# Decoder layer in emulated float32 on one core: the two down projections as seven half-size block products

## The chip, the cores and the metric

The kernel runs on one core of a Trainium2 chip. The metric is the device time of one execution in microseconds (us). A core has a matrix engine (PE, or TensorE), the vector engine DVE, the scalar engine ACT, the general engine POOL (GpSimd) and the engine SP, which here only issues transfers. Each works through its own instructions in a fixed order and waits on semaphores for the others; a transfer queued on SP holds everything queued behind it while it waits.

## The reference, cut to what matters

1024 tokens, width 1024, one layer: a SwiGLU half step, a token mixer, a second SwiGLU half step, each with a norm before and a norm behind it, and with shift, scale and gate rows made from a vector c.

```python
D_MODEL, SEQ, D_FF = 1024, 1024, 2816
def swiglu(h, w_gate, w_up, w_down):
    return (jax.nn.silu(h @ w_gate) * (h @ w_up)) @ w_down
# x += 0.5 * gate * rms_norm(swiglu(modulate(rms_norm(x))))   once before, once behind the mixer
# the nine rows (shift, scale, gate) x 3 are silu(c) @ w_mod + b_mod, w_mod being 1024 x 9216
```

The down projection is act (1024 x 2816) by w_down (2816 x 1024), in float32.

## The kernel before, in words

**Float32 by splits.** An operand is split into a high part, cast on ACT, and a low part, which DVE makes by a subtraction (`split`, L75; `psplit`, L79, makes it on POOL). `mm3` (L102) then issues three matmuls: high by high, high by low, low by high. A matmul here is always 128x128 by 128x512.

**Stages, in us of the profiled execution.** Opening to 130 (first gate/up products among it), gate/up 1 to about 490, its down projection to about 750, mixer to 1890, gate/up 2 to 2265, its down to about 2500, the last norm to the end.

**Gate/up** (`gate_up`, L252) is already made of seven half-size products. It goes over NB = 11 blocks of 256 columns of D_FF; each has seven steps i = 0..6 of 2 x 4 mm3. Step 2 makes the sums of weight blocks on POOL (L286 to L289), each step has weights split (`wl` on DVE), and DVE adds the products together out of PSUM (L343, L346). ACT takes the silu, POOL multiplies (L351), and SP stores one 128x512 tile of activations to DRAM for each of i = 1, 4, 5, 6 (L353). Operands are prepared LOOK steps ahead. Between the steps of the blocks from EARLY = 5 on, a generator `mod_rest` is advanced FILL = 2 times a step: it makes the rows for shift, scale and gate. For each half row it loads eight 128x512 pieces of w_mod (`wr`, four buffers, on SP) and accumulates them on DVE (`macc`, L183 and L185); then come a split, two matmuls with ones (bank `mo`) and one or two tiny DVE instructions on 1x512 (`junk`, L194 to L199). What is not done by the end of gate/up 1 runs in the second pass of down 1.

**Down** (`down`, L368) first loads all activations into SBUF (`act`, 44 loads of 256 KB, four chunks ahead of the products) and keeps them. It makes two passes over 22 chunks of 128 rows of w_down: output columns 0 to 511 for all eight token tiles, then columns 512 to 1023 for tiles 0 to 3 and for tiles 4 to 7. Each PSUM bank is read by ACT (sum of squares) and by DVE (times the gate row, `evac`, L363). Then `post1` or `post2` takes the norm of a half (four token tiles), adds the residual (`residual`, L1155) and, in the first layer, makes the mixer's input (`prenorm`, L1162). The last half's norm runs behind the last product. The mixer's first weights (`wc0r`) are loaded and split there (`wc0h` on ACT, `wc0l` on POOL).

**Order.** A scheduler builds each engine's order from the program order and each engine keeps it; tiles come from pools with fixed numbers of buffers, and a load into a buffer waits until the last reader of the tile before has ended.

Of the kernel before, what the change touches and what calls it, by code (L numbers as in the profile page):

```python
# [10 lines left out]
F32 = mybir.dt.float32  # L11
# [9 lines left out]
D = 1024  # L21
# [8 lines left out]
FILL = 2  # L30
NPT, NAP = 6, 6
# [8 lines left out]
class Layer:  # L40
# [125 lines left out]
    def mod_rest(self, pool, rows):  # L166

        nc, i = self.nc, self.i
        gains = {4: "g_pre_mix", 7: "g_pre_ffn2", 2: "g_post_ffn1", 5: "g_post_mix", 8: "g_post_ffn2"}
        for v in (2, 3, 4, 5, 6, 7, 8):  # L170
            for h in range(2):
                c0 = v * D + h * 512
                acc = pool.tile([P, 512], F32, name="macc")
                for k in range(8):
                    r = pool.tile([P, 512], F32, name="wr", tag="wr", bufs=4)
                    nc.sync.dma_start(r, i["w_mod"][0, k * P:(k + 1) * P, c0:c0 + 512])
                    if k == 4:
                        bt, gt = rows[0][0:1, :], rows[1][0:1, :]
                        nc.sync.dma_start(bt, i["b_mod"][0:1, c0:c0 + 512])
                        if v in gains:  # L180
                            nc.sync.dma_start(gt, i[gains[v]][0:1, h * 512:(h + 1) * 512])
                    if k == 0:
                        nc.vector.tensor_scalar(acc, r, self.scol[:, 0:1], None, op0=ALU.mult)  # L183
                    else:
                        nc.vector.scalar_tensor_tensor(acc, r, self.scol[:, k:k + 1], acc, op0=ALU.mult, op1=ALU.add)  # L185
                    yield
                b = self.bank("mo", tag=self.mo)
                ah = pool.tile([P, 512], F32R, name="mah", tag="wr", bufs=4)
                al = pool.tile([P, 512], F32R, name="mal", tag="wr", bufs=4)
                self.split(ah, al, acc)  # L190
                nc.tensor.matmul(b, self.ones, ah, start=True, stop=False)
                nc.tensor.matmul(b, self.ones, al, start=False, stop=True)
                if v in (4, 7):
                    nc.vector.scalar_tensor_tensor(bt, b[0:1, :], 1.0, bt, op0=ALU.add, op1=ALU.add)  # L194
                    nc.vector.tensor_mul(bt, bt, gt)
                else:
                    nc.vector.tensor_add(bt, b[0:1, :], bt)  # L197
                    if v in gains:
                        nc.vector.scalar_tensor_tensor(bt, bt, 1.0 if v == 5 else 0.5, gt, op0=ALU.mult, op1=ALU.mult)  # L199
                nc.sync.dma_start(self.rows[v:v + 1, h * 512:(h + 1) * 512], bt)  # L200
                yield
# [50 lines left out]
    def gate_up(self, W, raws, pools, V, wg, wu, actd):  # L252
# [44 lines left out]

        prepped = set()
# [18 lines left out]
        def steps(order, filler=None, ahead=()):  # L317
# [4 lines left out]
            for s, (b, i) in enumerate(order):  # L322
# [4 lines left out]
                for m in range(2):  # L327
# [5 lines left out]
                    if m == 0 and i < 4:  # L333
                        if i == 0 and b in early and b > 2:
                            tiles[b, i] = [pools["x"].tile([P, 512], F32, name="px", tag="wr", bufs=4) for _ in range(2)]
# [32 lines left out]
    def down(self, W, W2, wd, room, actd, y, G, junk, ss, post, filler=None):  # L368

        nc = self.nc  # L370
        NF = DFF // P
        tags = ("tr", "tr", "o", "gg", "pj", "pj", "s", "pt")
        got = [0]
        bg = iter(())
        for dh, tiles in ((0, range(8)), (1, range(4)), (1, range(4, 8))):
            bk = {t: self.bank("dn", tag=tags[t]) for t in tiles}
            halves = sorted({t // 4 for t in tiles})
            late, last = [], dh == 1
            nlate = (1, LATE + (W2 is not None) * 2 if tiles[-1] == 7 else 1)[dh]

            def mul(t, c, w, a):
                ts = slice((t % 4) * P, (t % 4 + 1) * P)
                ah, al = a[t // 4]
                self.mm3(bk[t], ah[:, ts], al[:, ts], w[0], w[1], c == 0, c == NF - 1)

            for c in range(NF):
                while got[0] < min(NF, c + 4):
                    for h in range(2):
                        nc.sync.dma_start(room[got[0]][h], actd[got[0], :, h * 512:(h + 1) * 512])
                    got[0] += 1  # L390
                if c % 2 == 0:
                    r = self.raw([P, 2, 512], "rd")
                    nc.sync.dma_start(r, wd[0, c * P:(c + 2) * P, dh * 512:(dh + 1) * 512]
# [1014 lines left out]
```

## Time and profile before

| | |
|---|---|
| median of three runs | 2530.2 us |
| the three runs | 2525.76, 2530.2, 8078.31 us |
| the profiled execution's own time | 2522.99 us |
| its span, first to last instruction | 2521.2 us |
| mean granted TensorE clock | 0.970 |
| busy: PE, DVE, ACT, POOL | 94%, 64%, 43%, 38% |
| matmuls | 11279 |

"Busy" says how much of the span an engine had an instruction in flight. As an average over unlike stages it doesn't tell what bounds any of them: for that, the busy times are taken stage by stage, and then the waits in the stage. A wait is named as "who waits <- who ended last", so that "PE gu L105 <- DVE wl L77" is PE standing until DVE had made the low part of a weight.

### The profile page before, as it was taken

Reading aid. Unit: us, or ns where it says so; the run is one execution under the profiler, and the core shown is the slowest. Engines: PE = TensorE matmul, PEld = TensorE weight load, DVE = VectorE, ACT = ScalarE, POOL = GpSimd, SP = SyncE. Lnnn points to the kernel's source line nnn. Section 1 sums busy time; section 2 is a strip of 40 time slices with the busy share of each in tenths; the row PEclk is TensorE's granted clock in tenths of the full one; section 3 lists DMA queues with packets and bytes.
Section 4 is the critical chain, followed back from the end, with each engine's and each line's share of the span. In section 5 each row is a group of like instructions: output and inputs, shape, how many; then the busy total and the mean of one; then the engine's idle time right before and its main releaser. Section 6 shows DMA issues by size and latency. Waiting matters only on the chain.

```text
span 2521.2 us, 33999 instructions
## 1 busy us (share of the span) xinstructions
PE 2362.8 (94%) x11279; PEld 1983.2 (79%) x11279; DVE 1611.2 (64%) x3193; ACT 1094.4 (43%) x2342; POOL 952.4 (38%) x1109
## 2 busy tenths in 40 slices
PE   5799999999999999999998899799879999999997
PEld 4578887788878878888997777678658888888886
DVE  7866778754884245999736388874486554553455
ACT  5422323233454355777453466623443333333443
POOL 5775555400005423432243144601587454430012
PEclk9899999999999999999998699999889999999999
DMA  9234555761633223513311422154234322253134
GB/s 282 85 109 134 152 153 159 241 219 51 193 131 119 74 88 109 187 30 89 117 31 59 118 70 65 44 200 167 84 113 130 96 76 92 80 193 108 52 108 150
DMA packets 229803, 300.04 MB, mean 119 GB/s; under 512 B 23606, under 2 KB 144342, under 8 KB 229628
## 3 DMA queue, kind: packets, MB, share of 16 engines
q1 hardware_dynamic: 228988, 296.80, 37.3%
q8 instruction: 90, 1.47, 0.2%
q10 hardware_dynamic: 640, 1.07, 0.1%
q14 instruction: 85, 0.70, 0.1%
HBM read 233.98 MB, written 63.83 MB: 118 GB/s over the span
## 4 chain that ended last, share of the span: by engine, by line
PE 69%; DVE 13%; DMA 8%; issue 4%; POOL 3%; ACT 2%; SPq 0%; DVEq 0%; POOLq 0%; ACTq 0%
PE gu L104 7%; PE gu L105 7%; PE gu L106 7%; PE dn L105 6%; PE dn L106 6%; PE dn L104 6%; DMA wr<-in_w_mod_dram 3%; PE gpj L104 2%; PE gpj L105 2%; PE gpj L106 2%; PE bq L104 2%; DVE macc L185 1%; PE bq L106 1%; PE bq L105 1%; DVE wl L77 1%
## 5 line engine op out<-in xcount | busy, mean ns | idle before, releaser
L104 PE MATMUL gu<-V,wh 128*128 128x512 f32 x1232 | 488.9, 397 | 18.9 <-ACT wh L76 9.3
L105 PE MATMUL gu<-V,wl 128*128 128x512 f32 x1232 | 487.9, 397 | 6.9 <-DVE wl L77 6.5
L106 PE MATMUL gu<-V,wh 128*128 128x512 f32 x1232 | 483.1, 395 | 4.5 <-DVE V L77 4.5
L77 DVE TENSOR_TENSOR wl<-rw,wh 128x512 fp32r<-128x512 f32 x232 | 215.3, 931 | 134.8 <-PE gu L105 95.4
L104 PEld LDWEIGHTS gu<-V,wh 128*128 128x128 f32 x1232 | 235.0, 191 | 73.3 <-ACT wh L76 11.3
L105 PEld LDWEIGHTS gu<-V,wl 128*128 128x128 f32 x1232 | 234.8, 191 | 60.4 <-DVE wl L77 9.4
L106 PEld LDWEIGHTS gu<-V,wh 128*128 128x128 f32 x1232 | 233.6, 190 | 56.6 <-DVE V L77 7.1
L105 PE MATMUL dn<-dh,al 128*128 128x512 f32 x704 | 275.3, 391 | 1.2 <-DVE al L77 1.1
L106 PE MATMUL dn<-dl,ah 128*128 128x512 f32 x704 | 274.0, 390 | 0.0
L104 PE MATMUL dn<-dh,ah 128*128 128x512 f32 x704 | 253.4, 391 | 6.5 <-DVE junk L197 6.5
L76 ACT CAST wh<-rw 128x512 fp32r<-128x512 f32 x232 | 140.1, 618 | 213.0 <-PE gu L106 124.9
L351 POOL TENSOR_TENSOR p<-p 128x512 f32<-128x512 f32 x86 | 129.9, 1511 | 246.5 <-ACT wh L81 78.5
L343 DVE TENSOR_TENSOR p<-gu,p 128x512 f32<-128x512 f32 x252 | 170.0, 681 | 68.9 <-PE gu L106 42.9
L76 ACT CAST ah<-act 128x512 fp32r<-128x512 f32 x176 | 107.4, 621 | 182.9 <-PE dn L105 132.9
L77 DVE TENSOR_TENSOR al<-act,ah 128x512 fp32r<-128x512 f32 x176 | 118.0, 689 | 81.5 <-PE dn L105 42.8
L104 PEld LDWEIGHTS dn<-dh,ah 128*128 128x128 f32 x704 | 132.3, 188 | 34.5 <-DVE junk L197 7.0
L105 PEld LDWEIGHTS dn<-dh,al 128*128 128x128 f32 x704 | 132.6, 188 | 29.9 <-DVE al L77 2.6
L77 DVE TENSOR_TENSOR dl<-rd,dh 128x512 fp32r<-128x512 f32 x132 | 91.2, 692 | 100.9 <-PE dn L105 52.5
L106 PEld LDWEIGHTS dn<-dl,ah 128*128 128x128 f32 x704 | 132.5, 188 | 27.6
L349 ACT ACTIVATE p<-p 128x512 f32<-128x512 f32 x86 | 54.4, 633 | 211.0 <-DVE p L343 161.7
L185 DVE SCALAR_TENSOR_TENSOR macc<-wr,scol,macc 128x512 f32<-128x512 f32 x98 | 93.3, 952 | 51.2 <-DMA wr<-in_w_mod_dram 50.5
L76 ACT CAST dh<-rd 128x512 fp32r<-128x512 f32 x132 | 81.6, 618 | 82.9 <-PE dn L105 71.5
(465 smaller groups left out, 5473.9 us busy)
## 6 DMA issues: line engine op xcount, KB each, us to landing
rd<-in_w_down_dram SPq DMA_DIRECT2D x66, 512.0 KB
wr<-in_w_mod_dram SPq DMA_DIRECT2D x112, 256.0 KB
rw<-in_w_gate_dram SPq DMA_DIRECT2D x44, 512.0 KB
rw<-in_w_up_dram SPq DMA_DIRECT2D x44, 512.0 KB
act<-act SPq DMA_DIRECT2D x88, 256.0 KB
act<-p SPq DMA_DIRECT2D x86, 256.0 KB
wm<-in_w_mod_dram SPq DMA_DIRECT2D x32, 256.0 KB
x<-xt SPq DMA_DIRECT2D x16, 512.0 KB
```

The costliest lines, as they stand in the source:

```text
L76: self.nc.scalar.copy(hi, src)
L77: self.nc.vector.tensor_sub(lo, src, f(hi))
L104: mm(out, ah, bh, start=start, stop=False)
L105: mm(out, al, bh, start=False, stop=False)
L106: mm(out, ah, bl, start=False, stop=stop)
L185: nc.vector.scalar_tensor_tensor(acc, r, self.scol[:, k:k + 1], acc, op0=ALU.mult, op1=ALU.add)
L343: nc.vector.tensor_tensor(x[m], bk, y[m], op=ALU.add)
L349: nc.scalar.activation(x[0], x[0], AF.Silu)
L351: nc.gpsimd.tensor_tensor(x[1], x[1], x[0], op=ALU.mult)
```

## The change

**Down as seven products.** act is cut into 2 x 2 blocks (token halves by even and odd chunks of D_FF) and w_down likewise (chunk parity by column halves). `down` now makes seven products of 11 chunks x 4 token tiles x mm3, in the order `prods`, with two sets of four banks in turn. Both operands are loaded from DRAM for two chunks at a time (`ra`, `rd`, 512 KB each), and split by ACT and DVE. Behind each product, `o1` to `o7` combine the banks into y: ACT copies, DVE additions, POOL subtractions; where a block of y is done, its square goes to ACT and its gate multiplication to POOL or DVE. The norm of half 0 runs under the last two products, that of half 1 behind the last.

**Operands of the seven products.** `operands` makes the sums of activation blocks at steps 1, 4, 5 and 6 of each gate/up block (three on POOL, one on DVE) and stores 7 tiles a block (8 in an early block, one of which is loaded again) instead of 4. `mix_down` makes the sums of w_down blocks in quarters of 128x256: for each of 11 chunk pairs and two column quarters q, two loads, four subtractions (POOL for q = 0, DVE for q = 1) and four stores, out of one buffer `wx`. It is advanced beside the steps of gate/up.

**Rows of shift, scale and gate.** `mod_rest` accumulates in place in the loaded tile (`wr`, five buffers), ends a half row DELAY = 3 loads later, and is advanced once a step in the early blocks too; in down 1 it is advanced once a chunk in the first five products.

```diff
+DELAY = 3
...
+                    acc = r
...
+        def operands(b, i, x):
+            out = lambda n, t: nc.sync.dma_start(ad[n, b], t)
+            sub = lambda E, o, x, y: E.tensor_tensor(o, x, y, op=ALU.subtract)
+            if i == 1:
+                tiles[b, "21"] = x
+                if b in early:
+                    out(7, x[1])
+                return
+            if i != 1:
+                tiles[b, {4: "22", 5: "12", 6: "11"}[i]] = x
+                out({4: 1, 5: 2, 6: 0}[i], x[1])
+            if i == 4:
...
+                nc.gpsimd.tensor_tensor(x[0], tiles[b, "21"][1], x[1], op=ALU.add)
+                out(3, x[0])
+            if i == 6:
+                (s1, _), (s3, a21), (s4, a12), (s2, a11) = (tiles[b, n] for n in ("22", "21", "12", "11"))
+                sub(nc.gpsimd, s2, s1, a11)
+                out(4, s2)
+                sub(nc.vector, s3, a11, a21)
+                out(5, s3)
+                sub(nc.gpsimd, s4, a12, s2)
+                out(6, s4)
...
-                            ff, h = {1: (0, 0), 4: (1, 0), 5: (1, 1), 6: (0, 1)}[i]
-                            nc.sync.dma_start(actd[2 * b + ff, :, h * 512:(h + 1) * 512], x[1])
-                if filler is not None and b >= len(early):
-                    for _ in range(FILL):
+                            operands(b, i, x)
+                if filler is not None:
+                    for _ in range(FILL if b >= len(early) else 1):
                         next(filler, None)
...
+    def mix_down(self, pool, wd, out):
+        for j in range(NB):
+            for q in range(2):
+                E = nc.vector if q else nc.gpsimd
+                r = pool.tile([P, 2, 2, 256], F32, name="wx", tag="wx", bufs=1)
+                for e in range(2):
+                    nc.sync.dma_start(r[:, e], wd[0, (2 * j + e) * P:(2 * j + e + 1) * P, :]
+                                      .rearrange("p (c f) -> p c f", c=2)[:, :, q * 256:(q + 1) * 256])
+                yield
...
+                sub(b11, b12, b11)
+                sub(b12, b22, b12)
+                sub(b22, b22, b11)
+                sub(b21, b22, b21)
+                yield
+                for n, t in enumerate((b11, b22, b12, b21)):
+                    nc.sync.dma_start(out[n, j, :, q * 256:(q + 1) * 256], t)
+                yield
...
+        def o6(b, t):
+            add(C(1, 2, t), C(1, 1, t), b)
+            nc.gpsimd.tensor_tensor(C(2, 1, t), C(1, 2, t), C(2, 1, t), op=ALU.subtract)
...
+        def o3(b, t):
+            add(C(1, 2, t), C(1, 2, t), b)
+            normed(1, 2, t, nc.gpsimd)
+        prods = [(0, wb[0, 0], o1), (1, T(3), o4), (4, T(1), o6), (3, T(0), o5), (5, T(2), o7),
+                 (2, wb[1, 0], o2), (6, wb[1, 1], o3)]
+        for n, (A, B, end) in enumerate(prods):
...
+            for j in range(NB):
+                if j % 2 == 0:
+                    m = min(2, NB - j)
+                    r = [raws(n, j).tile([P, 2, 512], F32, name=x, tag="raw") for x in ("rd", "ra")]
+                    nc.sync.dma_start(r[1][:, 0:m], ad[A, j:j + m].rearrange("j p f -> p j f"))
+                    nc.sync.dma_start(r[0][:, 0:m], B[:, j:j + m])
+                w, a = ([Ws(n, j).tile([P, 512], F32R, name=f"{m}{x}", tag="w") for x in "hl"] for m in "da")
+                self.split(a[0], a[1], r[1][:, j % 2])
+                self.split(w[0], w[1], r[0][:, j % 2])
...
+                if end in (o2, o3):
+                    next(bg, None)
+                elif filler is not None:
+                    next(filler, None)
...
+            for t in range(4):
+                for x in late:
+                    mul(t, *x)
+                end(bk[t], t)
...
-        with pool("cp") as cp, pool("wa", 16) as W, pool("ce") as ce, pool("r2", 4) as L.rawp, pool("tb") as tb:
+        with pool("wa", 16) as W, pool("r2", 4) as L.rawp, pool("cp") as cp, pool("ce") as ce, pool("tb") as tb:
```

**How the orders move.** DVE in gate/up 1, between two additions out of PSUM of block 6, before (`macc` are the row accumulations, `p` the additions, `wl` the weight splits):

```order
L343 TENSOR_TENSOR p3_2583<-gu_2570,p2_2539 128x512
L77 TENSOR_TENSOR wl0_2606<-rw01_2265,wh0_2605 128x512
L185 SCALAR_TENSOR_TENSOR macc_2750<-wr_2895,scol_99,macc_2750 128x512
L185 SCALAR_TENSOR_TENSOR macc_2750<-wr_2898,scol_99,macc_2750 128x512
L343 TENSOR_TENSOR p3_2583<-gu_2585,p2_2539 128x512
L77 TENSOR_TENSOR wl1_2610<-rw11_2267,wh1_2609 128x512
L185 SCALAR_TENSOR_TENSOR macc_2750<-wr_2938,scol_99,macc_2750 128x512
L343 TENSOR_TENSOR p0_2439<-gu_2617,p3_2583 128x512
```

The same stretch with the change (accumulation is into `wr_1923` and `wr_2354`, `wx` are the sums of w_down):

```order
L382 TENSOR_TENSOR p3_2495<-gu_2482,p2_2438 128x512
L203 SCALAR_TENSOR_TENSOR wr_1923<-wr_2242,scol_100,wr_1923 128x512
L78 TENSOR_TENSOR wl0_2526<-rw01_2155,wh0_2525 128x512
L419 TENSOR_TENSOR wx_2573<-wx_2573 128x256
L188 TENSOR_TENSOR junk0_96<-mo_2134,junk0_96 1x512
L203 SCALAR_TENSOR_TENSOR wr_1923<-wr_2294,scol_100,wr_1923 128x512
L382 TENSOR_TENSOR p3_2495<-gu_2497,p2_2438 128x512
L190 SCALAR_TENSOR_TENSOR junk0_96<-junk0_96,junk1_97 1x512
L201 TENSOR_SCALAR wr_2354<-wr_2354,scol_100 128x512
L78 TENSOR_TENSOR wl1_2530<-rw11_2157,wh1_2529 128x512
L203 SCALAR_TENSOR_TENSOR wr_1923<-wr_2347,scol_100,wr_1923 128x512
L203 SCALAR_TENSOR_TENSOR wr_2354<-wr_2404,scol_100,wr_2354 128x512
```

Between the two additions on p3, four instructions besides the split now stand where two stood, and the row accumulations of two half rows overlap.

SP in gate/up 1 with the change (before, only the `wr`, `rw` and `act1` rows are there):

```order
L415 DMA wx_2407<-in_w_down1_dram 128x2x256
L198 DMA wr_1523<-in_w_mod_dram 128x512
L311 DMA act1_85<-px_443 128x512
L426 DMA wx1_86<-wx_2407 128x256
L426 DMA wx1_86<-wx_2407 128x256
L198 DMA wr_1566<-in_w_mod_dram 128x512
L311 DMA act1_85<-px_442 128x512
L198 DMA wr_1610<-in_w_mod_dram 128x512
L426 DMA wx1_86<-wx_2407 128x256
L426 DMA wx1_86<-wx_2407 128x256
L311 DMA act1_85<-p3_2116 128x512
L415 DMA wx_2471<-in_w_down1_dram 128x2x256
```

The next load of `wx` stands behind the four stores out of the same buffer, and the weight and row loads queue among them.

DVE near the end of down 1 with the change, where the sixth product's banks are added (`y1 <- dn`) and the seventh's operands (`dl`, `al`) are split:

```order
L78 TENSOR_TENSOR al_6377<-ra_6371,ah_6376 128x512
L441 TENSOR_TENSOR y1_4537<-y1_4537,dn_5916 128x512
L1253 SCALAR_TENSOR_TENSOR xt_6163<-y0_4538,sums_4548,xt_6163 128x1024
L441 TENSOR_TENSOR y1_4537<-y1_4537,dn_5917 128x512
L441 TENSOR_TENSOR y1_4537<-y1_4537,dn_5918 128x512
L441 TENSOR_TENSOR y1_4537<-y1_4537,dn_5919 128x512
L78 TENSOR_TENSOR dl_6375<-rd_6370,dh_6374 128x512
```

The residual of the fourth token tile (`xt_6163`) stands ahead of a split that a later chunk needs; before, it stood among the splits of the second pass, without an addition behind it.

## Rows read from the trace of the kernel before

**Rows 1.** By stage: start:end, length, busy (xinstructions) by engine, clock, DMA share, GB/s

```profile
130.00:290.00 160.00, 159.63 (x691) 129.97 (x692) 101.37 (x138) 46.94 (x79) 102.51 (x71) 1.00 0.43 130
290.00:490.00 200.00, 198.87 (x861) 161.13 (x860) 164.50 (x210) 58.97 (x107) 109.62 (x68) 1.00 0.54 166
490.00:515.00 25.00, 18.45 (x74) 14.69 (x73) 12.33 (x20) 5.81 (x10) 3.26 (x3) 0.86 1.04 377
515.00:750.00 235.00, 234.82 (x1044) 193.25 (x1043) 153.13 (x287) 101.96 (x191) 0.00 (x0) 1.00 0.42 138
750.00:780.00 30.00, 23.06 (x115) 20.99 (x114) 24.95 (x82) 14.26 (x35) 17.23 (x28) 0.89 0.43 149
...
1890.00:2265.00 375.00, 374.64 (x1647) 309.60 (x1646) 206.51 (x268) 119.30 (x198) 187.60 (x141) 1.00 0.34 109
2265.00:2500.00 235.00, 233.86 (x1032) 193.31 (x1031) 111.51 (x168) 94.31 (x174) 18.96 (x38) 1.00 0.32 107
```

**Rows 2.** Costliest groups of the page: count | busy, mean ns | idle

```profile
L105 PE MATMUL dn<-dh,al 128*128 128x512 f32 x704 | 275.3, 391 | 1.2 <-DVE al L77 1.1
```

**Rows 3.** Waits of PE, 100 to 2522: total us, times, longest

```profile
PE dn L104 <- DVE junk L197: 6.5, 1, 6.5
PE gu L105 <- DVE wl L77: 6.5, 6, 2.1
...
PE cpj L104 <- ACT wc0h L81: 3.9, 1, 3.9
```

**Rows 4.** Waits, 300 to 480

```profile
DVE macc L185 <- DMA wr<-in_w_mod_dram: 20.0, 19, 2.2
...
DVE macc L183 <- DMA wr<-in_w_mod_dram: 12.1, 5, 3.9
```

**Rows 5.** DVE's groups by shape, 300 to 500

```profile
L185 DVE SCALAR_TENSOR_TENSOR macc<-wr,scol,macc 128x512 f32<-128x512 f32 x48 | 50.7, 1056 | 20.5 <-DMA wr<-in_w_mod_dram 20.3
L77 DVE TENSOR_TENSOR wl<-rw,wh 128x512 fp32r<-128x512 f32 x56 | 46.3, 829 | 0.0
L343 DVE TENSOR_TENSOR p<-gu,p 128x512 f32<-128x512 f32 x59 | 39.6, 679 | 0.0
L77 DVE TENSOR_TENSOR mal<-macc,mah 128x512 fp32r<-128x512 f32 x7 | 6.3, 893 | 0.9 <-ACT mah L76 0.7
...
L199 DVE SCALAR_TENSOR_TENSOR junk<-junk,junk 1x512 f32<-1x512 f32 x3 | 4.2, 1407 | 0.0
...
L197 DVE TENSOR_TENSOR junk<-mo,junk 1x512 f32<-1x512 f32 x5 | 3.3, 670 | 0.0
```

**Rows 6.** POOL's groups by shape, 300 to 500

```profile
L289 POOL TENSOR_TENSOR rw<-rw,rw 128x512 f32<-128x512 f32 x9 | 16.1, 1792 | 4.6 <-DVE wl L77 4.6
```

**Rows 7.** DVE's groups, 540 to 620, where POOL is idle

```profile
L77 DVE TENSOR_TENSOR al<-act,ah 128x512 fp32r<-128x512 f32 x29 | 18.9, 688 | 26.4 <-ACT ah L76 26.4
...
L185 DVE SCALAR_TENSOR_TENSOR macc<-wr,scol,macc 128x512 f32<-128x512 f32 x3 | 2.3, 752 | 2.4 <-DMA wr<-in_w_mod_dram 2.4
```

**Rows 8.** The chain that ended last, 380 to 520: start, us, what

```profile
408.02 4.11 DMA wr<-in_w_mod_dram
...
490.84 6.38 DMA act<-act
497.28 5.90 DMA rd<-in_w_down_dram
```

**Rows 9.** Waits of SP's queue, 120 to 560

```profile
SPq L353 <- POOL p L351: 113.8, 27, 9.2
...
SPq L176 <- DVE macc L185: 48.2, 47, 2.6
```

**Rows 10.** DVE's groups, gate/up 2, 1900 to 2260

```profile
L77 DVE TENSOR_TENSOR wl<-rw,wh 128x512 fp32r<-128x512 f32 x112 | 106.5, 951 | 123.2 <-PE gu L105 94.2 <-issue 12.4 <-ACT p L349 9.6
```

**Rows 11.** DVE's timeline, 753 to 780: start, us

```profile
755.94 1.26 DVE L1160 SCALAR_TENSOR_TENSOR xt<-y,sums,xt 128x1024 f32<-128x1024 f32 x1
```

**Rows 12.** DVE's timeline, 2505 to 2522

```profile
2511.48 0.68 DVE L366 TENSOR_TENSOR y<-dn,G 128x512 f32<-128x512 f32 x1
```

More of the change, by code (lines that the diff above doesn't have):

```diff
@@ new lines, in end @@
+        def end(v, h, acc):
+            c0 = v * D + h * 512
+            bt, gt = rows[0][0:1, :], rows[1][0:1, :]
+            nc.sync.dma_start(bt, i["b_mod"][0:1, c0:c0 + 512])
+            if v in gains:
+                nc.sync.dma_start(gt, i[gains[v]][0:1, h * 512:(h + 1) * 512])
+            b = self.bank("mo", tag=self.mo)
+            ah, al = (pool.tile([P, 512], F32R, name=f"ma{n}", tag="wr", bufs=5) for n in "hl")
+            self.split(ah, al, acc)
+            nc.tensor.matmul(b, self.ones, ah, start=True, stop=False)
+            nc.tensor.matmul(b, self.ones, al, start=False, stop=True)
+            if v in (4, 7):
+                nc.vector.scalar_tensor_tensor(bt, b[0:1, :], 1.0, bt, op0=ALU.add, op1=ALU.add)
+                nc.vector.tensor_mul(bt, bt, gt)
+            else:
+                nc.vector.tensor_add(bt, b[0:1, :], bt)
+                if v in gains:
+                    nc.vector.scalar_tensor_tensor(bt, bt, 1.0 if v == 5 else 0.5, gt, op0=ALU.mult, op1=ALU.mult)
+            nc.sync.dma_start(self.rows[v:v + 1, h * 512:(h + 1) * 512], bt)
@@ new lines, in mod_rest @@
+        late = None
+        for v, h in [(v, h) for v in (2, 3, 4, 5, 6, 7, 8) for h in range(2)]:
+            c0 = v * D + h * 512
+            for k in range(8):
+                r = pool.tile([P, 512], F32, name="wr", tag="wr", bufs=5)
+                nc.sync.dma_start(r, i["w_mod"][0, k * P:(k + 1) * P, c0:c0 + 512])
+                if k == 0:
+                    acc = r
+                    nc.vector.tensor_scalar(acc, r, self.scol[:, 0:1], None, op0=ALU.mult)
+                else:
+                    nc.vector.scalar_tensor_tensor(acc, r, self.scol[:, k:k + 1], acc, op0=ALU.mult, op1=ALU.add)
+                yield
+                if late and k == DELAY:
+                    end(*late)
+                    yield
+            late = v, h, acc
@@ L204, in turn @@
+        for _ in range(DELAY):
+            yield
+        end(*late)
     def turn(self, ys, d, sh, a=None):
@@ L366, in evac @@
         self.nc.vector.tensor_tensor(y, b, g, op=ALU.mult)
-    def down(self, W, W2, wd, room, actd, y, G, junk, ss, post, filler=None):
+    def mix_down(self, pool, wd, out):
         nc = self.nc
-        NF = DFF // P
-        tags = ("tr", "tr", "o", "gg", "pj", "pj", "s", "pt")
-        got = [0]
-        bg = iter(())
[L375 to L393, printed above, removed]
-                                      .rearrange("(k p) f -> p k f", p=P))
-                pool = W2 if W2 is not None and nlate > 1 and NF - nlate <= c < NF - nlate + 2 else W
-                w = [pool.tile([P, 512], F32R, name=f"d{n}", tag="w") for n in "hl"]
-                self.split(w[0], w[1], r[:, c % 2])
-                a = {}
-                for h in halves:
-                    a[h] = [pool.tile([P, 512], F32R, name=f"a{n}", tag="w") for n in "hl"]
-                    self.split(a[h][0], a[h][1], room[c][h])
-                if c >= NF - nlate:
-                    late.append((c, w, a))
@@ L404, in down @@
                     continue
[L405 to L407 removed]
+                for t in range(4):
+                    mul(t, j, w, a)
+                if end in (o2, o3):
                     next(bg, None)
[L409 to L414 removed]
@@ L422, in down @@
-        for _ in bg:
+                end(bk[t], t)
+            if end is o7:
+                bg = post(0)
+        for _ in post(1):
             pass
@@ L1182, in layer_kernel, with both @@
     sums = lambda: [L.const.tile([P, 4], F32, name="sums", bufs=8) for t in range(8)]
-    def rooms(fp):
-        r = [L.big.tile([P, 8, 512], F32, name="act", tag="big") for _ in range(4)]
-        f2 = [[fp[h].tile([P, 512], F32, name=f"act{c}{h}") for h in range(2)] for c in range(16, DFF // P)]
-        return [[r[2 * h + c // 8][:, c % 8] for h in range(2)] for c in range(16)] + f2
+    def both(a, b):
+        n = 0
+        while n < 2:
+            n = sum(next(g, 0) is not None for g in (a, b))
+            yield
+    operands = lambda n: L.dram.tile([8, NB, P, 512], F32, name=f"act{n}")
+    sums_of = lambda n: L.dram.tile([4, NB, P, 512], F32, name=f"wx{n}")
     L.turns = gu_turns()
```

150 lines of the change are left out of this document (82 added, 68 removed).

## The prediction

> **What bounds the kernel now.** I read the busy times by stage first, since a share over the whole span mixes stages with unlike limits. In both down projections PE is busy for 235 of 235 us at the full clock while DVE and ACT are at two thirds or under [rows 1]: down is bound by the number of its matmuls, and little else stands in it. Gate/up 2 is the same, with DVE busy 206.5 of 375 us. Gate/up 1 looks like that too, but from 290 to 490 DVE is at 164.5 of 200 us, and of its 35.5 idle us 32.1 are waits for pieces of w_mod [rows 1, 4]. The chain of waits confirms it: in that stretch it runs through DVE and through loads of `wr` of 4 us, not through PE [rows 8]. So PE and DVE are both nearly full there. Then I read the boundary from 490 to 515: 377 GB/s, PE busy 18.45 us, clock 0.86, the chain in loads of `act` and `rd` [rows 1, 8]. The question is whether work that down loses comes back in gate/up 1.
>
> **The change part by part.** Sums are made against the profiled execution, 2523.0 us; the median is 7.2 above it and the lowest run 2.8 above.
>
> *Fewer matmuls in down.* Before, 3 x 704 = 2112 of them [rows 2], 1056 a layer; with the change 7 x 11 x 4 x 3 = 924, so 264 fewer in all. From 515 to 750, 1044 take 235 us [rows 1], 0.2251 us each: **-59.4 us**. What feeds them: a product has 22 splits on DVE at 0.69 us [rows 7], 15 us in its 132 x 0.2251 = 29.7; additions behind a product are four to twelve, in another bank set than PE's next product. Covered, with half of DVE free.
>
> *Gate/up 1, DVE.* Counted in the order, DVE gets from the blocks behind the early ones: 25 more row accumulations at 1.056 us = 26.4; three more ends of a half row at 0.893 + 1.407 + 0.670 = 2.97, 8.9 [rows 5]; six subtractions of activation blocks, taken as 0.829 like a split in that stretch, 5.0; 24 subtractions of 128x256. Those the trace does not have. A 128x1024 instruction takes 1.26 us [rows 11] and a 128x512 one of that kind 0.752 [rows 7], so about 0.51 goes with 512 columns and 0.24 is fixed: 0.24 + 0.25 = 0.5, an estimate, x 24 = 12.0 (ends: half of 0.829, 10, and 0.829, 20). Together 52. POOL also gets about 16 sums at up to 1.79 us [rows 6] and 24 quarter sums at half of that plus, some 47 us, beside 109.6 [rows 1]. With POOL idle an accumulation takes 752 ns and a split 688; in this stretch they take 1056 and 829, while the additions out of PSUM stay at 679 [rows 5, 7]. That is 48 x 0.304 + 56 x 0.141 + 7 x 0.2 = 24 us of DVE for 109.6 us of POOL, 0.22 us for each: + 10. The Trainium skill ("SBUF - State Buffer", "Who interferes with whom") says that DVE with two SBUF inputs and GpSimd reading SBUF contend for one shared port as for a lock, the loser standing for the whole instruction; it speaks against this change. The trace agrees in kind (only the instructions with two SBUF inputs are longer) and not in size: 0.22, not one for one. By that rule the 10 us would be up to 47, a rival below.
>
> So DVE needs 164.5 + 62 = 226 us in a stretch of 200. Of its 32 us of waits half go: five buffers instead of four, and a busier DVE is waited for rather than waiting; half stay, since the loads queue on SP among twice as many transfers. 226 + 16 + the 3 other idle us = 245; less some 12 that operands prepared ahead and the early blocks take up, where DVE is busy for 101.37 of 160 us [rows 1]. **+33 us**. Low end +8: no wait left, the quarters at the low price, the rest in the early blocks. High end +55: all waits stay, quarters at 0.829. Behind a late addition out of PSUM stands the bank, so PE waits; it is already seen to wait 6.5 us for `wl` [rows 3].
>
> *Gate/up 2.* The same sums, without rows. DVE gets 44 quarters and 11 subtractions, about 32 us on 206.5 of 375, POOL 33 sums and 44 quarters, some 75 on 187.6 [rows 1]. DVE idles there 94 us waiting for PE [rows 10]: covered, **+2** (0 to +10, if that cover breaks up into pieces shorter than the sums).
>
> *Boundary to down 1.* The 44 loads of activations go; each product streams its own. 74 matmuls in 25 us are 16.7 us of work, so 8.3 were lost, 6.5 of them in one wait of PE for a `junk` of the rows [rows 1, 3]. With the change only two operands of 512 KB are wanted at once, but the last block's activations go to DRAM and back. **-5** (-9 to +5).
>
> *Residual of the fourth tile.* It stands on DVE ahead of a split and behind a load that queues on SP behind the mixer's weights, which wait for buffers that PE frees. If it is late, splits behind it are late and PE stands: a load of 4 us [rows 8] and 1.26 [rows 11], less what is split ahead. **+3** (0 to +6).
>
> *Boundary to the mixer.* Now 23.06 of 30 us [rows 1], 3.9 of it a wait for `wc0h` [rows 3]. The first mixer weights are split earlier, and half of the small norm instructions go to POOL: **-3** (-8, above the whole 6.9 lost; +4, if POOL is late with them).
>
> *Tail.* Behind the last bank an addition of 0.68 [rows 12] and then POOL's multiplication instead of DVE's alone: **+1** (0 to +3).
>
> *DMA.* Down reads 7 x 11 x 0.524 MB = 40.4 MB in 208 us, 194 GB/s, where it now has 138; at 490 to 515 the chip moved 377 [rows 1]. Nothing, unless that rate is not to be had (third rival).
>
> Sum: -59.4 + 33 + 2 - 5 + 3 - 3 + 1 = **-28**, 2495 for a profiled run; some 4 us more for a timed median: **2499 us**.
>
> **The rivals.** Within 2% means 2479.6 to 2580.8, about what a measurement of this kernel can tell.
>
> *The whole gain.* DVE's added work goes into its 32 us of waits and the early blocks, and PE hardly notices: +33 becomes about 0 and the mixer boundary gives 6. 2463 us. For it: DVE is idle for 59 us in the first stretch [rows 1] and the early blocks now take rows too. Against: the later blocks hold most of what is added, and PE already waits for DVE there [rows 3]. 0.22.
>
> *DVE locked out by POOL.* If all of the 47 us added on POOL stand in DVE's instructions, where 0.22 of them was taken, that is 37 us more: 2536. For it: the same instructions that are longer beside POOL are the ones added [rows 5, 7]. Against: the 0.22 measured there. 0.05. This is the rule of the Trainium skill named above, taken to its end.
>
> *Down paced by its loads.* If streams of two operands get only the 166 GB/s seen from 290 to 490 [rows 1], a down takes 243 us instead of 208: 2499 + 70 = 2569. For it: the first products also have rows and gate sums in the queue. Against: that stretch did not ask for more; 377 is seen. 0.08.
>
> *SP's queue behind the one buffer `wx` (slower).* A round is load, four subtractions, four stores, and the next load stands on SP until the stores have landed; all weight loads stand behind it. With 4.1 us for a load [rows 8] and 4.2 for a store's wait, 113.8 / 27 [rows 9], a round stands 8.3 us; 22 rounds a layer, 365 us in all. Loads are issued about three steps ahead, so most of it is hidden; it decides once the stands in a row exceed that lead. If a third shows, 122 us take the place of the 33 + 2 of DVE's term: 2499 - 35 + 122 = 2586. For it: SP's queue already waits long, 113.8 us and 48.2 on two kinds [rows 9]. Against: those waits cost PE almost nothing. 0.08.
>
> **How the numbers follow.** The forecast has 0.57. Its own range, from the ends of its terms (not all at one end), is 2470 to 2530. The range to hold the time 8 times in 10 takes in the whole gain below, 2463 less a few, and the lock-out and a part of the paced down above: **2456 to 2540**. Faster by over 2%: the whole gain's 0.22 and 0.01 of the forecast's lower end, 0.23. Slower: the queue's case, 0.08. Within: 0.56 + 0.05 + 0.08 = 0.69.
>
> **What would show it.** 1848 `dn` matmuls at 0.225 us each and down stages of 210 to 215 us show the first term. In gate/up 1's second half DVE over 90% busy, and PE waits for `wl` and for additions out of PSUM summing to 25 to 40 us, show the second; accumulations near 1.1 us show the contention. A boundary without a 350 GB/s burst shows the third. The forecast is wrong if gate/up 1 takes as long as before (whole gain), if PE's waits there end with loads of `rw` behind `wx` stores (queue), or if PE's waits in down end with `ra` or `rd` (paced).

## The result and the profile after

Median 2595.45 us against 2528.55 of the kernel before: a ratio of 1.0265 (95% interval 1.0249 to 1.028), **slower**, where 2499 with a range of 2456 to 2540 was forecast. One execution of either kernel was far slower (8078.31 us before, 4681.32 after) and is left out of the ratio. The profiled execution has a span of 2593.3 us, 72.1 more. By the first and last `gu` and `dn` matmul of the two timelines:

| | before | after | change | forecast |
|---|---|---|---|---|
| gate/up 1 ends | 496.5 | 569.0 | +72.4 | +33 |
| to the end of down 1 | 254.2 | 245.0 | -9.2 | -32 |
| mixer | 1067.6 | 1071.5 | +3.9 | -3 |
| gate/up 2 | 449.8 | 483.9 | +34.0 | +2 |
| down 2 | 240.8 | 209.4 | -31.4 | -30 |
| tail | 12.2 | 14.6 | +2.3 | +1 |

The busy times by stage of the changed kernel, to be read against [rows 1]:

```profile
130.00:290.00 160.00, 143.26 (x583) 114.14 (x582) 109.28 (x138) 38.33 (x67) 126.27 (x99) 0.94 0.66 214
290.00:490.00 200.00, 176.86 (x701) 136.27 (x700) 174.84 (x215) 45.16 (x82) 133.79 (x89) 0.95 0.69 222
...
580.00:620.00 40.00, 36.12 (x138) 28.17 (x137) 25.78 (x37) 15.45 (x29) 4.64 (x4) 0.88 0.98 343
620.00:740.00 120.00, 120.00 (x523) 97.72 (x522) 71.18 (x107) 55.44 (x99) 5.97 (x4) 1.00 0.61 196
740.00:815.00 75.00, 66.82 (x290) 53.35 (x289) 50.95 (x65) 37.38 (x80) 56.44 (x90) 0.98 0.49 158
2000.00:2200.00 200.00, 183.03 (x773) 144.55 (x772) 126.73 (x163) 50.55 (x92) 143.45 (x114) 0.99 0.57 186
2200.00:2360.00 160.00, 160.00 (x707) 132.50 (x706) 86.25 (x115) 51.42 (x84) 103.51 (x71) 1.00 0.34 112
2380.00:2560.00 180.00, 180.00 (x796) 149.07 (x795) 112.02 (x166) 90.78 (x173) 35.96 (x47) 1.00 0.65 228
```

The columns are those of [rows 1]. PE's busy share, about 89% in the first two rows, hides much; the counts behind it tell: 583 and 701 matmuls where 691 and 861 stood. In gate/up 2 PE is slow up to 2200 and at full pace behind it. Down, away from its boundaries, runs at 0.226 to 0.229 us a matmul with 196 to 228 GB/s.

In the second row 160 matmuls fewer are 37 us of PE at 0.231 us each. Of these 23.1 us are idle, by the waits of PE from 290 to 490:

```profile
PE gu L106 <- DVE wl L78: 9.0, 10, 3.2
PE mo L183 <- DVE mal L78: 5.1, 3, 2.1
PE mo L182 <- ACT mah L77: 4.7, 2, 3.7
PE gu L105 <- DVE p L385: 2.1, 1, 2.1
PE gu L105 <- DVE p L382: 2.0, 2, 1.2
```

Splits and additions out of PSUM make 13.1 us of it, the rows' own matmuls (`mo`) 9.8. The rest is matmuls that took longer: 176.86 us for 701, which at 0.231 would be 162. The granted clock is 0.95 there, where it was 1.00.

DVE's groups from 300 to 500, which answer to [rows 5]:

```profile
L203 DVE SCALAR_TENSOR_TENSOR wr<-wr,scol 128x512 f32<-128x512 f32 x57 | 67.4, 1183 | 16.8 <-DMA wr<-in_w_mod_dram 16.5
L78 DVE TENSOR_TENSOR wl<-rw,wh 128x512 fp32r<-128x512 f32 x47 | 40.6, 864 | 0.1
L382 DVE TENSOR_TENSOR p<-gu,p 128x512 f32<-128x512 f32 x47 | 31.9, 679 | 1.1 <-DMA act<-p 1.1
L419 DVE TENSOR_TENSOR wx<-wx 128x256 f32<-128x256 f32 x24 | 15.3, 639 | 2.0 <-DMA wx<-in_w_down_dram 1.6 <-issue 0.3
L78 DVE TENSOR_TENSOR mal<-wr,mah 128x512 fp32r<-128x512 f32 x8 | 9.1, 1138 | 0.0
```

The accumulation has gone from 1056 to 1183 ns with POOL busy 133.8 us instead of 109.6; the addition out of PSUM is still 679. The quarter sum, estimated at 0.5 us, took 0.639.

Waits of 2000 to 2200 (who <- on whom: us, times, longest):

```profile
DVE wx L419 <- DMA wx<-in_w_down_dram: 38.8, 8, 12.2
...
PE gu L106 <- DVE wl L78: 12.2, 12, 1.5
```

One of these eight, on DVE, on SP and on PE:

```profile
2166.43 1.18 DVE L78 TENSOR_TENSOR wl<-rw,wh 128x512 fp32r<-128x512 f32 x1
2178.01 0.43 DVE L419 TENSOR_TENSOR wx<-wx 128x256 f32<-128x256 f32 x1 [10.40 <-DMA wx<-in_w_down_dram]
2178.35 0.68 DVE L382 TENSOR_TENSOR p<-gu,p 128x512 f32<-128x512 f32 x1
```

```profile
2169.49 1.95 SPq L426 DMA_DIRECT2D wx<-wx  x3
2171.48 0.42 SPq L274 DMA_DIRECT2D rw<-in_w_gate_dram  x1
2172.95 1.20 SPq L415 DMA_DIRECT2D wx<-in_w_down_dram  x2
2178.46 3.26 SPq L426 DMA_DIRECT2D wx<-wx  x3
```

```profile
2179.18 0.47 PE L105 MATMUL gu<-V,wh 128*128 128x512 f32 x1 [1.08 <-DVE p L382]
2181.09 0.50 PE L106 MATMUL gu<-V,wl 128*128 128x512 f32 x1 [1.45 <-DVE wl L78]
```

DVE's next instruction is a sum whose load cannot be issued until POOL's round has left the one buffer. The last stores of POOL's round are issued by 2171.4, the load is issued at 2172.95 and has landed by 2178; DVE stands 10.40 us, with PSUM additions and weight splits behind it. PE still has work for most of that time; 2.5 us of it are lost behind those.

### The profile page after: what moved, and what is told of

It reads as the page before. It is cut to its first block, busy times and chain, and to the rows that moved or that the text cites. A ratio compares the mean times of both kernels' runs of the same rounds, so it can differ in the third digit from the quotient of the medians.

```text
span 2593.3 us, 34477 instructions
## 1 busy us (share of the span) xinstructions
PE 2350.3 (91%) x11015; PEld 1945.5 (75%) x11015; DVE 1739.6 (67%) x3225; ACT 1094.4 (42%) x2358; POOL 1237.2 (48%) x1397
## 5 line engine op out<-in xcount | busy, mean ns | idle before, releaser
L105 PE MATMUL gu<-V,wh 128*128 128x512 f32 x1232 | 499.8, 406 | 35.6 <-DVE p L382 17.1
L107 PE MATMUL gu<-V,wh 128*128 128x512 f32 x1232 | 490.8, 401 | 2.9 <-DVE V L78 2.9
L78 DVE TENSOR_TENSOR wl<-rw,wh 128x512 fp32r<-128x512 f32 x232 | 234.5, 1016 | 19.6 <-ACT wh L77 19.3
L106 PE MATMUL dn<-dh,al 128*128 128x512 f32 x616 | 241.0, 396 | 1.3 <-DVE al L78 1.3
L107 PE MATMUL dn<-dl,ah 128*128 128x512 f32 x616 | 232.7, 396 | 4.7 <-DVE dl L78 4.7
L78 DVE TENSOR_TENSOR al<-ra,ah 128x512 fp32r<-128x512 f32 x154 | 112.6, 736 | 91.5 <-ACT ah L77 91.4
L77 ACT CAST ah<-ra 128x512 fp32r<-128x512 f32 x154 | 94.8, 621 | 164.4 <-PE dn L106 128.5
L203 DVE SCALAR_TENSOR_TENSOR wr<-wr,scol 128x512 f32<-128x512 f32 x98 | 108.8, 1110 | 49.2 <-DMA wr<-in_w_mod_dram 48.8
L107 PEld LDWEIGHTS dn<-dl,ah 128*128 128x128 f32 x616 | 117.0, 190 | 31.0 <-DVE dl L78 6.0
L78 DVE TENSOR_TENSOR dl<-rd,dh 128x512 fp32r<-128x512 f32 x154 | 114.1, 746 | 30.2 <-ACT dh L77 16.5
L1156 POOL TENSOR_TENSOR aP<-aP,st 128x896 f32<-128x896 f32 (+3 forms) x64 | 74.2, 1170 | 112.9 <-DVE st L1155 107.4
```

The lines of the kernel that those rows point to most:

```text
L77: self.nc.scalar.copy(hi, src)
L78: self.nc.vector.tensor_sub(lo, src, f(hi))
L105: mm(out, ah, bh, start=start, stop=False)
L106: mm(out, al, bh, start=False, stop=False)
L107: mm(out, ah, bl, start=False, stop=stop)
L1156: nc.gpsimd.tensor_tensor(Pm, Pm, st[:, 1:2].to_broadcast([P, n]), op=ALU.mult)
```

## The experiments

Three suspects share gate/up: the sums of w_down, the sums of activation blocks, and the rows. Ratios are to the kernel before on the same chip. Runs that leave out work that the result needs (all but e3, e4, e8, e9, e10, e16 and e17) are for timing alone.

**First: leave out or undo one part.**

e1:

```diff
-        T = lambda n: wx[n].rearrange("j p f -> p j f")
+        T = lambda n: wb[1 - n % 2, 1]
...
-            fill, mix = L.mod_rest(wk, jkf), L.mix_down(fs, aps["w_down1"], wx)
+            fill, mix = L.mod_rest(wk, jkf), iter(())
```

> The sums of w_down blocks are left out (their loads, subtractions and stores beside gate/up); four of the seven products read a plain block of w_down in their place, so down's transfers and matmuls stay as many. In the changed kernel's trace gate/up 1 ends 72 us later than before and gate/up 2 takes 34 us longer. Theory R (the round of the single buffer wx: load, four subtractions, four stores, next load, with DVE, POOL and SP standing in order on its parts): gate/up 2 falls back by about 30 us and gate/up 1 by 35 to 50, the kernel to 2510 to 2530. Theory D (DVE's and POOL's added busy time, as predicted): 15 us of DVE and some 10 of contention are gone in gate/up 1, 5 to 10 in gate/up 2, the kernel at 2560.

Measured 2537.04, ratio 1.0034 (1.0021 to 1.0047): between the two theories and nearer to R. Gate/up 2 is back at 448.0 us, as R had it; gate/up 1 ends at 545.2, 24 us earlier where R had 35 to 50, and still 49 late.

e2: the three POOL and one DVE sums of `operands` deleted, plain tiles stored.

> The three sums on POOL and the one on DVE of activation blocks are left out; the seven stores a block stay and store plain tiles. Theory R: the w_down round remains, so little changes, 5 to 15 us off, 2580 to 2590. Theory D: POOL loses 25 us of two-input work from 300 to 560 and DVE 7, gate/up 1 shorter by 15 to 25 and gate/up 2 by 5 to 10, 2560 to 2570.

2592.31, 1.0261 (1.024 to 1.0281), little above R's range and far from D's; gate/up 1 ends at 564.5.

e3: `mod_rest` of before, advanced for `b >= EARLY` only.

> The rows of shift, scale and gate are made as before the change: a tile of their own for the accumulation, four load buffers, no delay of the end, and only beside the blocks from the sixth on; the rest runs in the first five products of down. Some 25 accumulations at 1.1 us and three ends at 3 us leave gate/up 1. Theory D: 30 to 40 us off gate/up 1, none off gate/up 2, 2555 to 2565. Theory R: most of that time is waited in the w_down rounds anyway, 5 to 20 us off, 2575 to 2590.

2600.6, 1.0292 (1.0271 to 1.0313); gate/up 1 ends at 567.0. This is above both ranges, and theory D's 2555 to 2565 falls: taking 25 accumulations out gave 2 us in gate/up 1 while the sums of w_down were there. (Gate/up 2, where nothing was edited, took 492.9 us instead of 483.9, so a few us in one stage prove little.)

e4: `mix` advanced once a step.

> Same work as the changed kernel, but the w_down sums are advanced once a step of gate/up throughout, not twice a step in the later blocks, so that the load, the subtractions and the stores of a round come one step of 5.4 us apart and the last blocks carry sums too. Theory R: the load (4 us) and the stores are then under a step's products; gate/up 2 gives back 20 to 30 us, gate/up 1 15 to 40, 2530 to 2560. Theory D: the work is the same, so the time is the same, 2590 to 2600 (a few us less if it is spread more evenly).

2598.59, 1.0276 (1.025 to 1.0302). This tells nothing between R and D: the scheduler took the sums as early as the buffer allowed all the same. In both kernels DVE and POOL have made the last sum of w_down by 500 us in layer 1 and by 2200 us in layer 2.

**Second: the round taken apart.**

e5: subtractions alone, on a resident tile.

> All 176 subtractions of the w_down sums stay on DVE and POOL in the same sizes, but on one resident tile: their loads and stores are left out (the products read plain blocks of w_down in their place). Without the sums altogether gate/up 2 was back at 448 us and the kernel at 2537; with all of them 484 and 2595. Theory R (an engine stands in order on the load of a round): nothing is waited for, 2535 to 2550. Theory D (the subtractions' busy time and their contention): most of the 58 us stay, 2575 to 2595.

2589.61, 1.0251 (1.0236 to 1.0266), as theory D had it; gate/up 2 474.6 us, gate/up 1 ends at 572.0.

e6: loads and stores alone.

> All loads and stores of the w_down sums stay, the subtractions are left out (plain blocks are stored). Theory R: SP still runs the rounds, one after the other, but no compute engine stands on a load: 2540 to 2560. Theory S (SP's queue: weight and row loads late behind the stores): the 58 us stay, 2580 to 2595. Theory D: 2540.

2568.2, 1.016 (1.0139 to 1.0182), between the ranges of R and S; gate/up 2 457.4 us, gate/up 1 ends at 570.0. In gate/up 2 the two halves cost 26.6 and 9.4 us of the 36; in gate/up 1 each of them alone costs the whole 24 us. Neither half is free, so R as I put it (the stand on the load alone) falls too. e5 is less clean than it looks: with no load to wait for, the sums were packed still closer. From 140 to 180 us DVE makes 34 of them in 28.7 us, where the changed kernel has 5 in 5.3. In e6 it is SP that stands, here from 130 to 290:

```profile
SPq L422 <- DMA wx<-in_w_down_dram: 28.3, 22, 3.2
SPq L415 <- DMA wx<-wx: 27.8, 25, 4.4
```

```profile
DVE p L382 <- DMA act<-p: 38.2, 7, 11.2
...
PE gu L105 <- DVE p L382: 16.7, 4, 5.7
```

The stores of activation tiles queue behind those 56 us of stands. DVE's next addition into such a tile waits until its store has landed, and PE waits for DVE.

e7: e1 and e3 together.

> The w_down sums are left out (as in the first run) and the rows of shift, scale and gate are made as before the change (as in the third, which alone changed nothing). In the first run's trace gate/up 1 still ended 49 us later than before, and its chain alternates loads of wr of 3 to 4.5 us with accumulations: the tiles px and the accumulators take buffers of wr. Theory B (the rows, advanced in the early blocks out of too few free buffers): gate/up 1 ends at 500 to 510, the kernel at 2490 to 2505. Theory O (the operand sums and the single p1 to p3 tiles held for them): gate/up 1 ends at 530 to 540, the kernel at 2525 to 2535.

2517.06, 0.9965 (0.995 to 0.998); gate/up 1 ends at 525.8, between the theories. The new rows do cost some 19 us where the old ones don't, and what they cost is read from e1's chain, 226 to 268:

```profile
229.33 4.53 DMA wr<-in_w_mod_dram
233.89 0.76 DVE wr L203
234.67 3.10 DMA wr<-in_w_mod_dram
237.86 1.07 DVE wr L203
238.94 2.72 DMA wr<-in_w_mod_dram
```

A load is issued only when the accumulation before it has ended. By the code, up to four tiles `px` of early blocks and the accumulator come out of the five buffers of `wr`, so hardly any is left to load ahead; before, the rows began when `px` was gone. No run gave `px` buffers of its own, so this reason for the chain is argued, not shown.

e8:

```diff
-                    E = nc.vector if t in (4, 6) else nc.gpsimd
+                    E = nc.vector
```

> The norm of layer 1 behind down (its tiny reciprocal square root instructions) all on DVE, as before the change, not on POOL. In the changed kernel's trace DVE waits 20 us for POOL's sums between 730 and 810, with splits of the seventh product behind it, and down 1 takes 237 us where 924 matmuls need 208. If that wait is the cause: down 1 shorter by 5 to 10 us, 2585 to 2590. If not (the splits wait for the PE anyway, or DVE becomes as late itself): 2593 to 2597.

2595.21, 1.0275 (1.0259 to 1.029). Down 1 itself took 229.6 instead of 237.3 us, as the wait on POOL had it; the mixer and gate/up 2 gave it back (1075.1 and 486.4 us), so the kernel's time is that of the second case.

**Third: pacing, and no rows at all.**

e9: `wx` shares the rotation of a gate/up tile, p2 of two buffers in layer 1 and p0 of four in layer 2, and `mix` advances once a step except in i = 0.

```diff
-                r = pool.tile([P, 2, 2, 256], F32, name="wx", tag="wx", bufs=1)
+                r = pool.tile([P, 2, 2, 256], F32, name="wx", tag=tag, bufs=nb)
```

> The w_down sums as in the changed kernel, but their buffers taken from the rotation of a gate/up tile (p2 in layer 1, p0 in layer 2, no more space), and advanced once a step except in each block's first: a round must wait for a tile that a block frees at its end, so about two rounds a block are possible and the sums spread over all blocks (in the changed kernel they are packed into the first half of gate/up). If packing is the cost: gate/up 2 from 484 to about 455 us and gate/up 1 5 to 20 us shorter, 2545 to 2565. If the sums cost their busy time wherever they stand: 2585 to 2600.

2578.05, 1.0207 (1.019 to 1.0224). It lies between the two expectations: gate/up 2 460.2 us, at full pace from 2040 on; gate/up 1 unmoved, 570.5.

e10: e9 with the old rows.

> The same, with the rows of shift, scale and gate made as before the change. Without any w_down sums these rows gave 2517 against 2537. If the costs in gate/up 1 are waits that overlap, taking away both is worth more than each: 2520 to 2550, gate/up 1 ending at 525 to 545. If the old rows are worth nothing as long as the sums are there, as in the third run: as the run before, 2545 to 2565.

2570.1, 1.0177 (1.016 to 1.0194); gate/up 1 ends at 559.2. The kernel is above both ranges: with the sums paced the old rows are worth 11 us in gate/up 1, not 25 or more.

e11 and e12: `mod_rest` replaced by one transfer of b_mod into the rows; e12 also without `mix_down`.

> The changed kernel without the rows of shift, scale and gate of w_mod (one transfer of b_mod fills them, so the output differs): no row loads, accumulations or ends in gate/up 1 and down 1. What is left in layer 1 is what layer 2 has. If the sums cost here what they cost there, gate/up 1 ends at 520 to 530 instead of 569 and down 1 takes 210 to 220 us, the kernel at 2525 to 2540. If the sums alone fill gate/up 1: 2570 to 2590.

> Neither rows nor w_down sums; the operand sums of activation blocks stay. If these are free where DVE and POOL have room, as in gate/up 2 of the first run: gate/up 1 ends at 485 to 495 and the kernel takes 2440 to 2460. If the held tiles p1 to p3 cost in layer 1 by themselves: gate/up 1 ends at 505 to 520, the kernel at 2465 to 2485.

2534.72 and 2463.95, 1.003 (1.002 to 1.004) and 0.9755 (0.974 to 0.977). Gate/up 1 ends at 522.4 and 492.4. e12 leaves work out and is no version to use, but it shows that the seven products are worth what was forecast (down 1 takes 27.6 us less than before, down 2 31.4, though down 1 has no rows here), and that the sums of activation blocks and the held tiles are free where rows are not made.

**Fourth: why rows and activation sums cost 33 us together and nothing alone.**

e13, and e14 with `nc.scalar` in its place:

```diff
-            out = lambda n, t: nc.sync.dma_start(ad[n, b], t)
+            out = lambda n, t: nc.gpsimd.dma_start(ad[n, b], t)
```

> The run without w_down sums and with the old rows (2517; gate/up 1 ends at 526, where it ends at 492 with neither rows nor w_down sums and at 497 before the change), with one thing moved: the stores of activation tiles and of their sums are issued by POOL, which makes them, not by SP. In that run's trace SP stands for three such stores from 340 to 357 while row loads queue behind them, and DVE then stands 6.1 us on a row load. Theory Q (SP's queue makes the row loads late): gate/up 1 ends at 500 to 512, the kernel at 2490 to 2503. Theory D (busy time of DVE and POOL together): as before, 2515 to 2530; if issuing costs POOL much, more.

> The same stores issued by ACT. SP no longer stands for POOL, but ACT does, with the casts of weights and the silu behind it. Theory Q, if ACT has the slack (30% busy there): 2490 to 2510; if ACT's stand takes the place of SP's: 2515 to 2530. Theory D: 2515 to 2520.

2544.17 and 2513.51, 1.0066 (1.0048 to 1.0084) and 0.9941 (0.9926 to 0.9956); gate/up 1 ends at 547.4 and 519.8. Off SP the stores gave 6 us when ACT issued them and lost 22 when POOL did. What issuing cost ACT was not separated, so 6 us is what this run shows of SP's queue, not a bound.

e15: e7 without the activation sums, stores kept.

> The run without w_down sums and with the old rows, and in addition without the four sums of activation blocks; the seven or eight stores a block stay, of plain tiles. Theory Q: a store then waits for the gating multiplication alone, as before the change, but still seven of them queue ahead of row loads: gate/up 1 ends at 500 to 515, 2490 to 2507. Theory D: POOL and DVE are as before, gate/up 1 at 497 to 505, 2485 to 2497. If the held tiles or the number of stores cost it: 526 stays.

2489.77, 0.9839 (0.9815 to 0.9864); gate/up 1 ends at 500.1. So it is the four sums, not the number of stores or the held tiles: 25.7 of the 33 us. Two things weaken that number: the profiled execution was 2478.76, 11 us under its median (the medians of e7 and e15 are 27.3 us apart), and without the sums SP has no sum to wait for either. From 290 to 490, for e7 and then e15:

```profile
290.00:490.00 200.00, 184.45 (x765) 142.87 (x763) 160.59 (x194) 50.50 (x93) 123.25 (x78) 0.99 0.52 160
```

```profile
290.00:490.00 200.00, 196.10 (x843) 159.00 (x842) 163.80 (x204) 55.75 (x101) 106.47 (x67) 0.99 0.56 174
```

DVE is no busier in e7 than before (164.50), and PE does 96 matmuls fewer than the 861 of [rows 1]. Its stands on row loads, 34.6 us here from 300 to 490, fill nearly all the rest, as 32.4 us of them did before: with rows DVE's time is nearly full, and 17 us more of POOL come on top. That this is the reason is argued; how it splits into longer instructions, late ones and SP's waits was not separated.

**Fifth: does the rest follow?** e18: e9 without rows.

> The changed kernel with the sums of w_down paced by the rotation of p2 and p0, and without the rows of shift, scale and gate (b_mod in their place). Unpaced, without rows, gate/up 1 ended at 522, with 492 if the w_down sums are left out too. With rows pacing gave nothing there (570.5 against 569.0). If it is the rows that leave the sums no room: gate/up 1 ends at 500 to 508 and gate/up 2 takes 460, the kernel at 2488 to 2500. If pacing does not work in layer 1 in any case: gate/up 1 at 518 to 525, 2505 to 2515.

2493.81, 0.9866 (0.9849 to 0.9883); gate/up 1 ends at 498.5. All sums are there, paced, with DVE 129 us busy:

```profile
290.00:490.00 200.00, 199.90 (x869) 162.92 (x868) 129.31 (x168) 57.84 (x103) 138.73 (x107) 1.00 0.49 157
```

e16: layer 1 as before, layer 2 with the seven products, paced.

> A version meant to be faster than both: the first layer as before the change, the second with the seven products, its w_down sums paced as in the run with the rotation of p0 (gate/up 2 at 460 us against 450 before, down 2 at 209 against 241, the tail 2 us longer). 2528 + 10 - 31 + 2 = 2509; 2500 to 2518.

2506.31, 0.991 (0.9893 to 0.9926). e17: e16 with its sums of w_down from gate/up 2's fourth block on.

```diff
-                if new and filler is not None and i:
+                if new and filler is not None and b >= 3:
                     next(filler, None)
```

> The version with the seven products in the second layer alone, its w_down sums begun at gate/up 2's fourth block, where in the run with all blocks the first two blocks lost most (PE 26.8 and 34.0 of 40 us at 1920 and 2000). If DVE and POOL have no room there for the sums beside the end of the mixer: gate/up 2 from 459 to 450 to 454, the kernel at 2496 to 2503. If the later blocks, with three rounds instead of two, lose as much: 2504 to 2510.

**2494.34**, 0.9863 (0.9841 to 0.9886): a complete kernel, some 33 us faster than before. That is 1.4%, clear of the interval but under the 2% that the verdict "faster" asks for. Gate/up 2 takes 448.9 us with all its sums:

```profile
1900.00:2060.00 160.00, 160.00 (x707) 132.53 (x707) 106.83 (x134) 50.41 (x84) 129.40 (x94) 1.00 0.51 167
2060.00:2260.00 200.00, 200.00 (x884) 165.65 (x883) 134.44 (x164) 62.31 (x103) 151.99 (x115) 1.00 0.53 171
```

## Why the prediction was wrong, step by step

**Fewer matmuls: right.** Down 2 lost 31.4 us for 29.7 forecast. Down's transfers ran at 196 to 228 GB/s and PE's waits name neither `ra` nor `rd`, so the rival of a down paced by its loads is out (down 2 took 209.4 us, not 243).

**Gate/up 1, DVE: this step failed, and in its last subtraction.** For the stretch of 861 matmuls it came to 245 us before "less some 12 that operands prepared ahead and the early blocks take up". At the rate measured, 701 in 200 us, 861 take 246. That this part came out is partly luck. By these rows DVE is busy 215 of the 246 us, not 226, at accumulations of 1183 instead of 1056 ns. It was busy 87% of the time where over 90 was named as the sign, and PE's waits for splits and additions were 13 us, not 25 to 40. What filled the gap, PE's waits for the rows' own matmuls and its lower clock, had no term. The early blocks, which were to absorb 12 us, lost 30 instead: 583 matmuls in the 160 us that held 691, so 691 take 190. e1 and e11 show both causes there, each alone: 640 matmuls with rows and no w_down sums, 642 with these and no rows. Their rows, and that of e5:

```profile
130.00:290.00 160.00, 151.29 (x640) 121.65 (x639) 100.27 (x135) 43.67 (x74) 116.20 (x81) 0.97 0.53 168
```

```profile
130.00:290.00 160.00, 151.81 (x642) 121.03 (x642) 98.88 (x128) 39.46 (x69) 127.14 (x103) 0.99 0.62 197
```

```profile
130.00:290.00 160.00, 136.38 (x560) 108.01 (x559) 128.25 (x152) 35.17 (x61) 140.16 (x114) 0.94 0.45 140
```

DVE is idle for 60 us in the first two. I took idle time as room. Room needs operands that have landed when the work's turn comes; the buffers that decide it (one `wx`; five `wr` less the tiles `px`) stood in the diff, and no term of the sum was made of them. But that is not all. In the changed kernel the longest of DVE's waits from 130 to 290 is a third one, for the stores of activation tiles, first before and then after:

```profile
DVE p L343 <- DMA act<-p: 6.0, 2, 5.3
```

```profile
DVE p L382 <- DMA act<-p: 18.6, 7, 7.0
```

And e5, whose sums wait for their first load alone, has the fewest matmuls, 560: there the sums stand packed ahead of what PE needs. How the 30 us split into late loads, late stores and packed sums stays open; the runs show that the rows or the sums of w_down bring a loss each, and that without both (e12) 693 matmuls stand there.

**Gate/up 2: the same mistake, +34 for +2.** "Covered", by 94 us of DVE waiting for PE [rows 10]. The cover was real (e17: 448.9 us), but the sums were packed into the first half, round after round through one buffer.

**The rival on SP's queue had the place and the size, and in part the waiter.** It gave 2586 for a third of the rounds showing. The chain load, sums, stores, load is what e9 and e17 loosened. In the scene shown from gate/up 2 it is DVE that stands in order on the load, while weight loads pass on SP at 2171.48. In gate/up 1, though, e6's rounds without their sums make SP stand 56 of 160 us and cost as much as the whole change's (570.0 against 569.0), with the stores of activation tiles late behind them. e13 and e14 have no rounds and say nothing of this. Its chance of 0.08 was too low for a chain that could be read in the order of SP's instructions.

**The lock-out rival** was not needed: beside POOL at 67% the accumulation stands at 1183 ns, 431 above its 752 with POOL idle [rows 7]. Counted like the 24 us of the prediction, accumulations, splits and `mal` of these 200 us make 57 x 0.431 + 47 x 0.176 + 8 x 0.450 = 36 us, 12 more, where 10 was put in and 47 by the rival. The Trainium skill ("SBUF - State Buffer", "Who interferes with whom") is again borne out in kind. The prediction read the rows too narrowly, however: not only instructions with two SBUF inputs are longer. The first multiplication of a half row, with one 128x512 tile as input, took 488 ns from 515 to 750 before, with POOL idle, and 901 from 300 to 500 after:

```profile
L183 DVE TENSOR_SCALAR macc<-wr,scol 128x512 f32<-128x512 f32 x4 | 2.0, 488 | 3.3 <-DMA wr<-in_w_mod_dram 3.3
```

```profile
L201 DVE TENSOR_SCALAR wr<-wr,scol 128x512 f32<-128x512 f32 x8 | 7.2, 901 | 1.6 <-DMA wr<-in_w_mod_dram 1.6
```

**Down 1: -9 for -32.** Nothing was counted for the rows that move under it. Without rows (e11) it takes 226.3 us and starts 0.2 us behind gate/up 1, against 237.3 and 7.7: 18.5 us. The boundary's burst did not go either, 343 GB/s from 580 to 620 with PE at 138 matmuls in 40 us. The norm on POOL cost 7.7 us by e8: DVE waited for it 20 us, at residuals (`xt`) and at the mixer's input (`y`), with splits behind. The fourth tile's residual, for which +3 stood, was not among these; it ran at 781.29 without a wait.

```profile
DVE y L1263 <- POOL sums L96: 12.9, 4, 6.1
...
DVE xt L1253 <- POOL sums L96: 7.3, 3, 3.0
```

**Mixer and tail.** Where the mixer's +3.9 for -3 and the tail's +2.3 for +1 lie was not followed; over the runs the mixer took 1068 to 1075 us.

## What to carry to other kernels

Idle time of an in-order engine is room for added work only if the work's operands are there at its turn, and if the work is not packed ahead of what the main loop needs (e5). For each added transfer write down the buffer it loads into, who frees it and how long the round is, and compare the round with the rate at which the order asks for it. A scheduler that takes work as early as it may packs it; to spread it, tie its buffer to one that the main loop frees at the pace wanted (e9, e17), since moving it in the program moved little (e4). Where one engine's time is nearly full, two additions that are each free can cost tens of us together: test them in pairs.

## What the runs showed of the hardware

A 128x256 sum of two SBUF tiles took 639 ns on DVE in gate/up 1, more than half of a 128x512 (864). In e5, from 130 to 490, it took 872. Issuing a 256 KB store from POOL's queue (e13) occupied POOL 566 ns each:

```profile
L302 POOL DMA_DIRECT2D act<-p x51 | 28.9, 566 | 8.8 <-DVE p L303 5.8 <-POOL p L381 1.2 <-POOL p L303 0.9
```

These are 180 to 490; the accumulation there took 1239 ns, against 1070 with the same stores on ACT (e14), and gate/up 1 ended 22 us later than with them on SP.

A stop of PE can also cost clock. In the changed kernel PE is busy for 3.50 of the 10 us from 270 on. In the next 10 the granted clock is 0.55, most of it the lower of its two levels (1.2 of 2.4 GHz), and 18 matmuls take 7.02 us, 0.39 each instead of 0.231:

```profile
270.00:280.00 10.00, 3.50 (x16) 2.54 (x14) 10.00 (x13) 1.66 (x3) 7.31 (x5) 0.94 0.57 189
280.00:290.00 10.00, 7.02 (x18) 5.55 (x19) 10.00 (x11) 3.80 (x7) 6.85 (x6) 0.55 0.55 183
```
